# Down projection of a decoder layer: steps run in pairs, product by product, with sums kept in PSUM

## The chip, the cores and the metric

The kernel runs on one core of a Trainium2 chip. The metric is the time of the whole program on the device in microseconds (us); of several executions the median is taken. The core's engines are TensorE (PE in the profile: matrix products, sums kept in PSUM banks of 128x512 f32), VectorE (DVE), ScalarE (ACT), GpSimd (POOL) and SyncE (SP, which here only issues DMAs). All but PE read and write SBUF; DVE and ACT also read PSUM.

## The reference

One layer of a decoder, batch 1, 1024 positions, width 1024, in f32:

```
h = rmsnorm(x); proj = h @ w_in
o = [rmsnorm(fox_attention), rmsnorm(stick_breaking_attention)]     # 8 + 8 heads of 64
x = x + o @ w_out
h = rmsnorm(x)
u = causal_dwconv(h @ w_up, conv_w, conv_b)                         # 1024 -> 2 x 2816, width 3
gate, val = split(u)
x = x + (silu(gate) * val) @ w_down                                 # 2816 -> 1024
out = rmsnorm(x)
```

The change concerns the last product, `(silu(gate) * val) @ w_down`, and the addition of x to it.

## The kernel before

Everything is held transposed: rows of a tile are features, columns are positions. An f32 matrix product is made of three matmuls on halves split as high + low part (`mm3`, L158 to L161: high x high, low x high, high x low). `wh` is the high part of a weight, cast by ACT (L904), and `wl` the low part, raw minus high, a subtraction on DVE or POOL (L906). The operands (b11, t2, t4, ... with h and l) are split in the same way by ACT (L760) and DVE or POOL (L761).

Up and down projection use a 2x2 block scheme with seven products in place of eight, and sums on both sides. A step is one pair of output row blocks: seven products, named in `PORD` (L49) by the weight block or weight sum they use: a11, s2, a22, a12, s1, s3, s4. Their other operand is, in that order, b11, t2, t4, b21, t1, t3, b22. The weight sums s1, s2, s3, s4 are made by POOL (L878, L879, L885, L886) from the raw weights `wraw`, which come by DMA from HBM (L863), in a pool of 2 buffers; the sums stand in the pool `sp_` with one buffer each.

- Up: 22 steps (`NJ`), products of 4 x 3 = 12 matmuls each. For each step the four outputs are put together by DVE, convolved (L1003), gated (L1098, `tg`), and stored in HBM as operands of the down projection (`td`).
- Down: the inner dimension comes in three chunks (`KN` = 4, 3, 3 blocks) and each chunk has four steps, 12 steps in all: 28 products of 12 matmuls and 56 of 9. After that comes a small plain part for the last two blocks (`plain`), and the final norm.

The loop over down steps (L1126 on) makes, for each product in the order of `PORD`, one call of `product`, which takes a fresh PSUM bank (`bank`, six of pool ps_u and two of ps_p in turn). Its result is added into the accumulators `y[m, c]` in SBUF by DVE. A copy of a11's result (`m1s`, by ACT) and a running sum `u2` serve several outputs; a step has 11 additions on DVE. The accumulators are loaded with x from HBM in `load_y` (L1118). Their pool `fin` takes the memory of the pool `up`, which the up phase and the staging of the operands of chunk 0 have used, so that the loads wait for the last use of it.

In the last step of the up phase and of a chunk, `operands` loads the operand for product n of the next chunk right after the last product n of the old one, through six staging buffers (`ua`, `ffr`, `m1s`), since the operands have one buffer each. `ahead_to(idx + 4)` has the weights of a product split four products ahead of its matmuls, in pair tiles for two products, three of them; which engine takes a `wl` stands in `produce`.

SP issues its DMAs in program order (L72). The order on the other engines is made by a scheduler, which may move instructions within their dependences.

Of the kernel before, what the change touches and what calls it, by code (L numbers as in the profile page):

```python
# [9 lines left out]
F32 = mybir.dt.float32  # L10
# [3 lines left out]
ALU = mybir.AluOpType  # L14
# [3 lines left out]
P = 128  # L18
# [8 lines left out]
NPRE = 3  # L27
# [41 lines left out]
def layer(ctx, tc, xT, wqk, wv0, wv, wout, wup, wdn, cols, fbias, yT):  # L69
# [3 lines left out]

    const = ctx.enter_context(tc.tile_pool(name="const", bufs=1))
    dram = ctx.enter_context(tc.tile_pool(name="dram", bufs=1, space=DRAM))
    wraw = ctx.enter_context(tc.tile_pool(name="wraw", bufs=2, side="right"))
    wspl = ctx.enter_context(tc.tile_pool(name="wspl", bufs=3, side="right"))

    ident = const.tile([P, P], F32, name="ident")
# [75 lines left out]
                    if d == 1:  # L155
                        n.split(min(n.pieces, int(frac * n.pieces + 0.01)))

    def mm3(ps, ah, al, bh, bl, start, stop):  # L158
        nc.tensor.matmul(ps, ah, bh, start=start, stop=False)  # L159
        nc.tensor.matmul(ps, ah, bl, start=False, stop=False)  # L160
        nc.tensor.matmul(ps, al, bh, start=False, stop=stop)  # L161

    small = ctx.enter_context(tc.tile_pool(name="small", bufs=4))

# [551 lines left out]

    x2x = ExitStack()
    b1p = ctx.enter_context(tc.tile_pool(name="b1p", bufs=1))
    sp_ = ctx.enter_context(tc.tile_pool(name="sp_", bufs=1))
    x2p = x2x.enter_context(tc.tile_pool(name="x2p", bufs=1))  # L720
    ps_u = ctx.enter_context(tc.tile_pool(name="ps_u", bufs=6, space=PSUM))

# [91 lines left out]
    tp_ = ctx.enter_context(tc.tile_pool(name="tblk", bufs=1, side="right"))  # L814
    t2, t4, t1, t3, b22 = (halves(tp_, n) for n in ("t2", "t4", "t1", "t3", "b22"))

    def product(w, o, b, n=4):
        ps = bank()
        wh, wl = w
        for k in range(n):  # L820
            sl = slice(o + k * P, o + (k + 1) * P)
            mm3(ps, wh[:, sl], wl[:, sl], b[k][0], b[k][1], k == 0, k == n - 1)
        return ps

    steps = [("u", j, 4) for j in range(NJ)] + [(c, mp, KN[c]) for c in range(NCH) for mp in range(KT // 2)]
# [18 lines left out]
    first(1)  # L844
    first(2)

    stream = [(j, n) for j in range(NS) for n in PORD if j >= NPRE or n not in ("a11", "a12")]
    made, tiles, plain = {}, {}, {}
    pos = [0]

# [272 lines left out]
    spare = [t[n] for n in range(KN[1], 4) for t in (b11, t2, t4, b21, t1, t3)]  # L1123
    rest = {}

    for s in range(NJ, NS):  # L1126
        c, mp, kn = steps[s]
        ev, od_ = 2 * mp, 2 * mp + 1
        for n in PORD:
            ahead_to(idx + 4)  # L1130
            if s == NS - 1 and n == PORD[3]:
                plain_split(0)
            if s == NS - 1 and n == PORD[-1]:
                plain_split(1)
            w, o = made[s, n]
            idx += 1
            ps = product(w, o, bmat[n], kn)
            if c == 0 and n == PORD[0]:
                if mp == 0:
                    load_y(0)  # L1140
                elif mp < KT // 2 - 1:
                    load_y(mp + 1)
            if c == 0 and mp == 0 and n == PORD[3]:
                load_y(1)
            if n == "a11":
                m1s = fin.tile([P, 512], F32, name="m1s")
                nc.scalar.copy(m1s, ps)
                tt(y[ev, 0], y[ev, 0], m1s, ALU.add)
            elif n == "s2":
                u2 = fin.tile([P, 512], F32, name="u2")  # L1150
                tt(u2, ps, m1s, ALU.add)
                tt(y[ev, 1], y[ev, 1], u2, ALU.add)
            elif n == "a22":
                tt(y[od_, 0], y[od_, 0], ps, ALU.subtract)
            elif n == "a12":
                tt(y[ev, 0], ps, y[ev, 0], ALU.add)
            elif n == "s1":
                tt(y[od_, 1], ps, y[od_, 1], ALU.add)
                tt(y[ev, 1], ps, y[ev, 1], ALU.add)
            elif n == "s3":  # L1160
                tt(u2, ps, u2, ALU.add)
                tt(y[od_, 1], y[od_, 1], u2, ALU.add)
                tt(y[od_, 0], y[od_, 0], u2, ALU.add)
            elif n == "s4":
                tt(y[ev, 1], ps, y[ev, 1], ALU.add)
            if mp == KT // 2 - 1 and c < NCH - 1:
                operands(n, c + 1, False)
            if c == 1 and mp == 1 and kind[n] < 4:
# [126 lines left out]
```

## Time and profile before

| | |
|---|---|
| median of 3 runs | 1442.48 us (1440.78 to 1443.48) |
| profiled execution | 1441.58 us, of which the span is 1439.6 us |
| mean granted clock of TensorE | 0.964 |
| busy, share of the span | PE 92%, DVE 78%, POOL 60%, ACT 43% |
| DMA queues by kind | hardware_dynamic 193.04 + 0.64 MB, instruction 0.85 + 0.36 MB |

The page's shares are averages over stages: the input projection and attention up to about 736 us, the up projection from there to 1174, the down projection to 1394, and the plain part with the final norm to 1440. Times on the span's scale start at 0 with the first instruction. A timeline row has the start, the time of one, engine, line, operation, output<-inputs, and in brackets how long the engine stood idle before and which work ended it. A wait row has engine, line, what was waited for, us in total, times, and the longest. In the table of stretches the clock is the share of full speed that TensorE was granted.

### The profile page before, as it was taken

What the parts mean: (1) busy time and instruction counts of PE and PEld (TensorE: products, weight loads), DVE (VectorE), ACT (ScalarE), POOL (GpSimd) and SP (SyncE); (2) the same over time, 40 slices, a digit from 0 to 9 for tenths busy, and PEclk for the clock granted to TensorE, in tenths of its full rate; (3) what the DMA queues carried; (4) which work ended last, traced back from release to release, by engine and by line L of the source; (5) the groups of instructions that cost most, each with busy time, mean ns of one, the idle gap of its engine ahead of it and who ended that gap; (6) DMA issues with size and microseconds to landing.
All of it is one profiled execution on the core that took longest, in us unless ns stands there. A gap on an engine that the chain in (4) does not pass through costs nothing.

```text
span 1439.6 us, 19147 instructions
## 1 busy us (share of the span) xinstructions
PE 1317.6 (92%) x6640; PEld 1075.9 (75%) x6640; DVE 1116.7 (78%) x1588; ACT 620.8 (43%) x1128; POOL 859.4 (60%) x730
## 2 busy tenths in 40 slices
PE   7899999999898887889778899999999998999995
PEld 5878878877787765777556688888888865878785
DVE  6246555655676677786899999998888889899987
ACT  5134434444454554353443434443443354344334
POOL 7344454543747573455667788878878763454423
PEclk9999999999999999999889999999999998999997
DMA  5556555545444454547311233333322355554313
GB/s 179 183 161 187 152 154 163 147 147 135 149 121 124 119 159 143 179 147 270 125 44 59 84 106 110 110 110 110 110 97 95 96 176 204 180 171 132 126 36 117
DMA packets 97232, 194.89 MB, mean 135 GB/s; under 512 B 8680, under 2 KB 35688, under 8 KB 97136
## 3 DMA queue, kind: packets, MB, share of 16 engines
q1 hardware_dynamic: 96272, 193.04, 42.6%
q8 instruction: 52, 0.85, 0.3%
q10 hardware_dynamic: 864, 0.64, 0.1%
q14 instruction: 44, 0.36, 0.1%
HBM read 132.79 MB, written 60.85 MB: 135 GB/s over the span
## 4 chain that ended last, share of the span: by engine, by line
PE 50%; DMA 18%; DVE 16%; POOL 7%; issue 6%; SPq 2%; ACT 2%; DVEq 0%; POOLq 0%; ACTq 0%
PE u L161 8%; PE u L160 8%; PE u L159 8%; PE pj L159 5%; PE pj L161 5%; PE pj L160 5%; DMA q<-qkd 4%; DVE fbt L493 3%; DMA vd<-vs 3%; DMA wraw<-in_wqk_dram 2%; DMA wraw<-in_wv_dram 2%; PE tp L505 2%; DMA fbt<-nfd 2%; PE o L526 2%; PE o L525 1%
## 5 line engine op out<-in xcount | busy, mean ns | idle before, releaser
L143 POOL TENSOR_TENSOR wl<-wraw,wh 128x256 fp32r<-128x256 f32 (+2 forms) x134 | 125.3, 952 | 26.9 <-ACT wh L140 21.3
L494 POOL TENSOR_TENSOR w<-w,fbt 128x128 f32<-128x128 f32 (+3 forms) x64 | 90.1, 1417 | 84.4 <-DVE fbt L493 59.9
L904 ACT CAST wh<-s 128x512 fp32r<-128x512 f32 (+1 forms) x136 | 79.8, 591 | 125.7 <-POOL s L879 71.0
L493 DVE TENSOR_TENSOR_SCAN fbt<-fbt 128x128 f32<-128x128 f32 (+3 forms) x64 | 103.5, 1624 | 25.9 <-ACT fbt L480 22.0
L142 POOL TENSOR_SCALAR wh<-wraw 128x256 fp32r<-128x256 f32 (+1 forms) x112 | 55.3, 509 | 108.8 <-DMA wraw<-in_wqk_dram 60.7
L878 POOL TENSOR_TENSOR s<-wraw 128x512 f32<-128x512 f32 (+1 forms) x34 | 55.8, 1641 | 96.0 <-DVE wl L906 53.5
L505 PE MATMUL tp<-ident,w 128*128 128x128 f32 x576 | 94.0, 281 | 19.5 <-DVE pl L514 9.5
L159 PE MATMUL pj<-xh,wh 128*128 128x512 f32 x224 | 103.1, 460 | 5.1 <-DVE yf L293 5.1
L906 POOL TENSOR_TENSOR wl<-wraw,wh 128x512 fp32r<-128x512 f32 x60 | 102.9, 1722 | 0.6 <-ACT wh L904 0.6
L505 PEld LDWEIGHTS tp<-ident,w 128*128 128x128 f32 x576 | 70.7, 144 | 39.1 <-DVE pl L514 12.6
L906 POOL TENSOR_TENSOR wl<-s,wh 128x512 fp32r<-128x512 f32 x48 | 88.5, 1845 | 13.8 <-ACT wh L904 13.4
L514 DVE TENSOR_TENSOR pl<-tp,ph 128x512 fp32r<-128x512 f32 x96 | 64.9, 685 | 40.9 <-ACT ph L513 40.5
L161 PE MATMUL pj<-xh,wl 128*128 128x512 f32 x224 | 91.9, 410 | 0.0
L160 PE MATMUL pj<-xl,wh 128*128 128x512 f32 x224 | 91.3, 407 | 0.0
L485 ACT ACTIVATE w<-w,m 128x128 f32<-128x128 f32 (+3 forms) x64 | 49.7, 776 | 91.1 <-DVE m L475 86.0
L1003 DVE SCALAR_TENSOR_TENSOR tg<-ua,col,tg 128x1023 f32<-128x1023 f32 (+1 forms) x44 | 88.1, 2002 | 0.0
L480 ACT ACTIVATE fbt<-s 128x512 f32<-128x512 f32 (+2 forms) x96 | 47.8, 498 | 83.8 <-PE s L470 39.2
L489 POOL TENSOR_SCALAR w<-w,l 128x128 f32<-128x128 f32 (+3 forms) x64 | 47.6, 748 | 59.9 <-DVE l L488 32.7
L904 ACT CAST wh<-wraw 128x512 fp32r<-128x512 f32 (+1 forms) x96 | 55.1, 589 | 63.1 <-DMA wraw<-in_wdn_dram 25.0
L1003 DVE SCALAR_TENSOR_TENSOR tv<-ub,col,tv 128x1023 f32<-128x1023 f32 (+1 forms) x44 | 76.0, 1727 | 5.7 <-ACT tv L1001 5.6
L513 ACT CAST ph<-tp 128x512 fp32r<-128x512 f32 x96 | 55.7, 590 | 53.1 <-PE o L525 33.4
L885 POOL TENSOR_TENSOR s<-wraw 128x512 f32<-128x512 f32 (+1 forms) x34 | 56.4, 1658 | 35.7 <-DVE wl L906 33.4
(409 smaller groups left out, 4569.4 us busy)
## 6 DMA issues: line engine op xcount, KB each, us to landing
wraw<-in_wup_dram SPq DMA_DIRECT2D x47, 512.0 KB, 3.6
qkd<-hl SPq DMA_DIRECT2D x32, 512.0 KB, 2.9
td<-tg SPq DMA_DIRECT2D x44, 256.0 KB, 2.3
vd<-vs SPq DMA_DIRECT2D x32, 256.0 KB, 4.5
q<-qkd SPq DMA_DIRECT2D x16, 512.0 KB
kh<-qkd SPq DMA_DIRECT2D x32, 256.0 KB, 16.6
kl<-qkd SPq DMA_DIRECT2D x32, 256.0 KB, 17.4
vt<-vd SPq DMA_DIRECT2D x16, 512.0 KB, 17.9
```

The costliest lines, as they stand in the source:

```text
L143: nc.gpsimd.tensor_tensor(self.lo[:, sl], self.raw[:, sl], f32(self.hi[:, sl]), ALU.subtract)
L159: nc.tensor.matmul(ps, ah, bh, start=start, stop=False)
L160: nc.tensor.matmul(ps, ah, bl, start=False, stop=False)
L161: nc.tensor.matmul(ps, al, bh, start=False, stop=stop)
L493: nc.vector.tensor_tensor_scan(qt[:, rev], qt[:, rev], qt[:, rev], 1.0, ALU.mult, ALU.bypass)
L494: nc.gpsimd.tensor_tensor(w[:, :n], w[:, :n], qt[:, T - n + 1:T + 1], ALU.mult)
L505: nc.tensor.transpose(tp[:, a * 256 + b * P:a * 256 + (b + 1) * P], ws[2 * g + b][:, kb * P:(kb + 1) * P], ident)
L514: nc.vector.tensor_tensor(pl[:, z:], tp[:, z:], f32(ph[:, z:]), ALU.subtract)
L885: nc.gpsimd.tensor_tensor(d["s3"], g[:, :w], v[:, :w], ALU.subtract)
L904: nc.scalar.copy(h[:, o:o + w], src)
L906: eng.tensor_tensor(l[:, o:o + w], src, f32(h[:, o:o + w]), ALU.subtract)
L1003: nc.vector.scalar_tensor_tensor(t[:, s:], us[:, :T - s], col[:, cw + tap:cw + tap + 1], t[:, s:], op0=ALU.mult, op1=ALU.add)
```

## The change

Two down steps of a chunk (two pairs of output row blocks) form a unit, and go product by product: product n of the first step, product n of the second, then the next n. The order of the products is new (`PORD_D`). Three of the seven go on accumulating in a bank that another product has begun (`ONTO`): s2 on a11's, s4 on s1's, s3 on a11's again. The copy `m1s` and the sums `u2` go: a step has 8 additions on DVE, and no ACT copy. The products a22 and a12 take banks of ps_p, the others of ps_u. y is loaded in the first unit, at positions 0, 1, 6 and 10. Raw weights of both steps of the next unit are asked for at a12. `wraw` gets four buffers and `sp_` two, and the DMA scratch of the program is set to 1024. The number of matmuls is the same.

```diff
+PORD_D = ("a11", "a22", "s1", "s2", "a12", "s4", "s3")
+ONTO = {"s2": "a11", "s4": "s1", "s3": "a11"}
-    wraw = ctx.enter_context(tc.tile_pool(name="wraw", bufs=2, side="right"))
+    wraw = ctx.enter_context(tc.tile_pool(name="wraw", bufs=4, side="right"))
-    sp_ = ctx.enter_context(tc.tile_pool(name="sp_", bufs=1))
+    sp_ = ctx.enter_context(tc.tile_pool(name="sp_", bufs=2))
...
-    def product(w, o, b, n=4):
-        ps = bank()
+    def product(w, o, b, n=4, onto=None, pool=None):
+        ps = onto or (pool.tile([P, 512], F32, name="u" if pool is ps_u else "pj") if pool else bank())
...
-            mm3(ps, wh[:, sl], wl[:, sl], b[k][0], b[k][1], k == 0, k == n - 1)
+            mm3(ps, wh[:, sl], wl[:, sl], b[k][0], b[k][1], k == 0 and onto is None, k == n - 1,
+                onto is not None)
...
+    units = [(j,) for j in range(NJ)] + [(j, j + 1) for j in range(NJ, NS, 2)]
+    stream = [(j, n) for q in units for n in (PORD if q[0] < NJ else PORD_D) for j in q
+              if j >= NPRE or n not in ("a11", "a12")]
...
         if n == ("a12" if j >= NPRE else "a22"):
-            raws(j + 1)
+            for q in follow[j]:
+                raws(q)
...
+    for unit in units[NJ:]:
+        c, _, kn = steps[unit[0]]
+        last = steps[unit[-1]][1] == KT // 2 - 1
+        on = {}
+        for at, (n, s) in enumerate((n, s) for n in PORD_D for s in unit):
...
+            ps = on[s, n] = product(w, o, bmat[n], kn, on.get((s, ONTO.get(n))),
+                                    pool=ps_p if n in ("a22", "a12") else ps_u)
+            if c == 0 and unit[0] == NJ and at in (0, 1, 6, 10):
+                load_y((0, 1, 6, 10).index(at))
+            if n in ("a11", "a12"):
+                tt(y[ev, 0], ps, y[ev, 0], ALU.add)
             elif n == "a22":
                 tt(y[od_, 0], y[od_, 0], ps, ALU.subtract)
...
+            elif n in ("s2", "s4"):
+                tt(y[ev, 1], ps, y[ev, 1], ALU.add)
+            else:
                 tt(y[od_, 1], ps, y[od_, 1], ALU.add)
...
+                if n == "s3":
+                    tt(y[od_, 0], ps, y[od_, 0], ALU.add)
+            if s != unit[-1]:
+                continue
+            if last and c < NCH - 1:
                 operands(n, c + 1, False)
...
-    nc = _bacc.Bacc("TRN2", target_bir_lowering=False, num_devices=1)
+    nc = _bacc.Bacc("TRN2", target_bir_lowering=False, num_devices=1,
+                    dynamic_dma_scratch_size=1024)
```

The scheduler's order moves in three places that matter below. In the rows a name has the number of its buffer, so one name with one number is one piece of memory. `[waits ...]` names the engines and DMA queues whose progress an instruction waits for.

First, PE in the first down unit. Before, the second product of the first step, s2 on t2, has a bank of its own, `u_11322`, beside a11's `u_11300`:

```order
L159 MATMUL u_11300<-b11h3_7182,wh_11120 128x512 [waits Activation_49]
L160 MATMUL u_11300<-b11l3_7183,wh_11120 128x512 [waits DVE_49]
L161 MATMUL u_11300<-b11h3_7182,wl_11121 128x512
L159 MATMUL u_11322<-t2h0_7624,wh_11120 128x512 [waits Activation_49]
L160 MATMUL u_11322<-t2l0_7625,wh_11120 128x512 [waits Pool_49]
L161 MATMUL u_11322<-t2h0_7624,wl_11121 128x512
```

In the changed kernel s2 comes after a11, a22 and s1 of both steps, and writes into a11's bank, `u_11298` (`u_11409` is s1 of the second step):

```order
L164 MATMUL u_11409<-t1h2_7644,wl_11290 128x512
L162 MATMUL u_11409<-t1h3_7646,wh_11289 128x512
L163 MATMUL u_11409<-t1l3_7647,wh_11289 128x512
L164 MATMUL u_11409<-t1h3_7646,wl_11290 128x512
L162 MATMUL u_11298<-t2h0_7624,wh_11343 128x512 [waits DVE_49,Activation_49]
L163 MATMUL u_11298<-t2l0_7625,wh_11343 128x512
L164 MATMUL u_11298<-t2h0_7624,wl_11344 128x512 [waits Pool_49]
```

The first of these matmuls has a wait for DVE, since DVE reads the same bank.

Second, DVE in the same place: `b22l1` to `b22l3` are the last operands staged through the old memory, `tg` is the last gated block, and y0_0 the first accumulator. Before:

```order
L761 TENSOR_TENSOR t3l3_7655<-m1s_11227,t3h3_7654 128x512 [waits DMAHW0_49,Activation_49]
L1003 SCALAR_TENSOR_TENSOR tg_11270<-ua_11137,col_76,tg_11270 128x1022 [waits DVE_49]
L906 TENSOR_TENSOR wl_11339<-wraw_11235,wh_11338 128x512 [waits PE_49,DMAHW2_49,Activation_49,Pool_49]
L906 TENSOR_TENSOR wl_11379<-s2_11381,wh_11378 128x512 [waits PE_49,Activation_49]
L906 TENSOR_TENSOR wl_11379<-wraw_11233,wh_11378 128x512 [waits DMAHW1_49]
L1098 TENSOR_TENSOR tg_11270<-tg_11270,tv_11266 128x1024 [waits Activation_49]
L761 TENSOR_TENSOR b22l1_7659<-ua_11251,b22h1_7658 128x512 [waits DMAHW4_49,Activation_49]
L761 TENSOR_TENSOR b22l2_7661<-ffr_11258,b22h2_7660 128x512 [waits DMAHW5_49,Activation_49]
L761 TENSOR_TENSOR b22l3_7663<-m1s_11262,b22h3_7662 128x512 [waits DMAHW6_49,Activation_49]
```

In the changed kernel, from the same t3l to the add that reads a11's bank:

```order
L764 TENSOR_TENSOR t3l3_7655<-m1s_11224,t3h3_7654 128x512 [waits DMAHW2_49,Activation_49]
L764 TENSOR_TENSOR b22l1_7659<-ua_11244,b22h1_7658 128x512 [waits DMAHW4_49,Activation_49]
L764 TENSOR_TENSOR b22l2_7661<-ffr_11251,b22h2_7660 128x512 [waits DMAHW5_49,Activation_49]
L1017 SCALAR_TENSOR_TENSOR tg_11263<-ua_11141,col_76,tg_11263 128x1022 [waits DVE_49]
L764 TENSOR_TENSOR b22l3_7663<-m1s_11255,b22h3_7662 128x512 [waits DMAHW6_49,Activation_49]
L919 TENSOR_TENSOR wl_11290<-s1_11316,wh_11289 128x512 [waits Pool_49]
L1112 TENSOR_TENSOR tg_11263<-tg_11263,tv_11259 128x1024 [waits Activation_49]
L919 TENSOR_TENSOR wl_11344<-s2_11317,wh_11343 128x512 [waits PE_49,Pool_49]
L919 TENSOR_TENSOR wl_11382<-wraw_10995,wh_11381 128x512 [waits PE_49]
L919 TENSOR_TENSOR wl_11382<-wraw_10999,wh_11381 128x512
L1157 TENSOR_TENSOR y0_0_11273<-u_11298,y0_0_11273 128x512 [waits DMAHW3_49,DMAHW7_49,DVE_49,Pool_49]
```

The three b22l have moved ahead of the weight splits and the gate product, and the add into y0_0 reads the bank itself and stands behind four wl.

Third, POOL at the start of the up projection (`_7801` to `_7803` are the sums of step 0, `_7920` to `_7922` those of step 1). Before:

```order
L878 TENSOR_TENSOR s1_7801<-wraw_7797 128x512
L879 TENSOR_TENSOR s2_7802<-s1_7801,wraw_7799 128x512
L885 TENSOR_TENSOR s3_7803<-wraw_7799,wraw_7797 128x512
L906 TENSOR_TENSOR wl_7796<-s2_7802,wh_7795 128x512
L906 TENSOR_TENSOR wl_7796<-wraw_7797,wh_7795 128x512
L886 TENSOR_TENSOR s2_7802<-wraw_7799,s2_7802 128x512
L906 TENSOR_TENSOR wl_7902<-s2_7802,wh_7901 128x512
L878 TENSOR_TENSOR s1_7920<-wraw_7820 128x512
L906 TENSOR_TENSOR wl_7943<-wraw_7820,wh_7942 128x512
```

In the changed kernel:

```order
L898 TENSOR_TENSOR s3_7803<-wraw_7799,wraw_7797 128x512
L891 TENSOR_TENSOR s1_7920<-wraw_7820 128x512
L892 TENSOR_TENSOR s2_7921<-s1_7920,wraw_7822 128x512
L898 TENSOR_TENSOR s3_7922<-wraw_7822,wraw_7820 128x512
L919 TENSOR_TENSOR wl_7796<-s2_7802,wh_7795 128x512
L919 TENSOR_TENSOR wl_7796<-wraw_7797,wh_7795 128x512
L899 TENSOR_TENSOR s2_7802<-wraw_7799,s2_7802 128x512
L919 TENSOR_TENSOR wl_7902<-s2_7802,wh_7901 128x512
L919 TENSOR_TENSOR wl_7902<-s2_7921,wh_7901 128x512
L891 TENSOR_TENSOR s1_8032<-wraw_7946 128x512
L899 TENSOR_TENSOR s2_7921<-wraw_7822,s2_7921 128x512
L919 TENSOR_TENSOR wl_7943<-wraw_7820,wh_7942 128x512
```

Three sums of step 1 now stand ahead of the first wl of step 0, and `wl_7943` (a22 of step 1) has s1 of step 2 and s4 of step 1 ahead of it. PE's own order is the same in the up projection.

## Rows read from the trace of the kernel before

**Rows 1.** The page's chain that ended last, shares of the span by engine.
```profile
PE 50%; DMA 18%; DVE 16%; POOL 7%; issue 6%; SPq 2%; ACT 2%; DVEq 0%; POOLq 0%; ACTq 0%
```

**Rows 2.** Table of stretches, PE: from:to, length, busy (matmuls), clock, DMA share, GB/s.
```profile
738.00:774.00 36.00, 26.71 (x84) 0.81 0.17 59
804.00:828.00 24.00, 19.68 (x75) 0.93 0.35 118
830.00:1174.00 344.00, 344.00 (x1481) 1.00 0.32 107
1174.00:1231.00 57.00, 47.03 (x169) 0.91 0.60 208
1231.00:1282.00 51.00, 51.00 (x221) 1.00 0.55 180
1394.00:1440.00 46.00, 29.47 (x186) 0.82 0.26 92
```

**Rows 3.** Timeline of PE: start, us of one, engine, line, operation, operands.
```profile
1174.31 0.39 PE L159 MATMUL u<-b11h,wh 128*128 128x512 f32 x1
1195.05 0.63 PE L159 MATMUL u<-t1h,wh 128*128 128x512 f32 x1
1231.27 0.40 PE L159 MATMUL u<-b11h,wh 128*128 128x512 f32 x1
1332.33 0.40 PE L159 MATMUL u<-t2h,wh 128*128 128x512 f32 x1
1350.31 0.40 PE L159 MATMUL u<-b11h,wh 128*128 128x512 f32 x1
```

**Rows 4.** Waits of PE, 1205 to 1400: line, releaser, us in total, times, longest.
```profile
PE pj L161 <- DVE wl L906: 2.9, 2, 2.7
PE pj L160 <- POOL b22l L761: 1.1, 1, 1.1
```

**Rows 5.** Waits of SP's DMA queue, 1150 to 1216.
```profile
SPq L1118 <- DVE b22l L761: 9.0, 1, 9.0
```

**Rows 6.** Timeline of SP's DMA queue at the loads of y.
```profile
1212.97 0.32 SPq L1118 DMA_DIRECT2D y<-x2f  x1
```

**Rows 7.** Timeline of DVE around the transition to the down projection.
```profile
1198.54 0.68 DVE L761 TENSOR_TENSOR t3l<-m1s,t3h 128x512 fp32r<-128x512 f32 x1
1200.94 1.76 DVE L761 TENSOR_TENSOR t3l<-m1s,t3h 128x512 fp32r<-128x512 f32 x1
1202.63 2.29 DVE L1003 SCALAR_TENSOR_TENSOR tg<-ua,col,tg 128x1022 f32<-128x1022 f32 x1
1208.80 2.30 DVE L1098 TENSOR_TENSOR tg<-tg,tv 128x1024 f32<-128x1024 f32 x1
1215.78 0.69 DVE L1148 TENSOR_TENSOR y<-y,m1s 128x512 f32<-128x512 f32 x1
```

**Rows 8.** Timeline of POOL at the start of the up projection.
```profile
735.00 1.75 POOL L885 TENSOR_TENSOR s<-wraw 128x512 f32<-128x512 f32 x1
738.54 1.81 POOL L906 TENSOR_TENSOR wl<-s,wh 128x512 fp32r<-128x512 f32 x1 [1.80 <-ACT wh L904]
747.93 9.53 POOL L906 TENSOR_TENSOR wl<-s,wh 128x512 fp32r<-128x512 f32 x1 [4.21 <-ACT wh L904]
757.43 1.71 POOL L878 TENSOR_TENSOR s<-wraw 128x512 f32<-128x512 f32 x1
```

**Rows 9.** Waits of PE, 738 to 774.
```profile
PE pj L161 <- POOL wl L906: 3.0, 1, 3.0
```

**Rows 10.** Waits of PE, 804 to 828.
```profile
PE pj L161 <- POOL wl L906: 2.2, 1, 2.2
PE u L161 <- DVE wl L906: 1.4, 1, 1.4
PE u L161 <- POOL wl L906: 0.5, 1, 0.5
```

**Rows 11.** Waits of POOL, 730 to 832.
```profile
POOL s L878 <- DMA wraw<-in_wup_dram: 9.5, 3, 3.7
```

More of the change, by code (lines that the diff above doesn't have):

```diff
@@ L156, in ahead, with mm3 @@
                         n.split(min(n.pieces, int(frac * n.pieces + 0.01)))
[L158 to L161, printed above, removed]
+    def mm3(ps, ah, al, bh, bl, start, stop, more=False):
+        nc.tensor.matmul(ps, ah, bh, start=start, stop=False, skip_group_check=more)
+        nc.tensor.matmul(ps, ah, bl, start=False, stop=False, skip_group_check=more)
+        nc.tensor.matmul(ps, al, bh, start=False, stop=stop, skip_group_check=more)
     small = ctx.enter_context(tc.tile_pool(name="small", bufs=4))
@@ L845, in layer @@
     first(2)
-    stream = [(j, n) for j in range(NS) for n in PORD if j >= NPRE or n not in ("a11", "a12")]
+    units = [(j,) for j in range(NJ)] + [(j, j + 1) for j in range(NJ, NS, 2)]
+    stream = [(j, n) for q in units for n in (PORD if q[0] < NJ else PORD_D) for j in q
+              if j >= NPRE or n not in ("a11", "a12")]
+    follow = {}
+    for q, r in zip(units, units[1:] + [(NS,)]):
+        if len(q) == len(r):
+            follow.update({j: (i,) for j, i in zip(q, r)})
+        else:
+            follow.update({j: () for j in q})
+            follow[q[-1]] = r
     made, tiles, plain = {}, {}, {}
@@ L1124, in layer @@
     rest = {}
[L1126 to L1129, printed above, removed]
+    for unit in units[NJ:]:
[3 more added lines that the diff above has]
+        for at, (n, s) in enumerate((n, s) for n in PORD_D for s in unit):
+            mp = steps[s][1]
+            ev, od_ = 2 * mp, 2 * mp + 1
             ahead_to(idx + 4)
[L1131 to L1134, printed above, removed]
+            if s >= NS - 2 and at in (10, 12):
+                plain_split(at // 2 - 5)
@@ L1135, in layer @@
             w, o = made[s, n]
             idx += 1
[L1137 to L1152, printed above, removed]
+            ps = on[s, n] = product(w, o, bmat[n], kn, on.get((s, ONTO.get(n))),
+                                    pool=ps_p if n in ("a22", "a12") else ps_u)
@@ L1153, in layer @@
+            if c == 0 and unit[0] == NJ and at in (0, 1, 6, 10):
+                load_y((0, 1, 6, 10).index(at))
+            if n in ("a11", "a12"):
+                tt(y[ev, 0], ps, y[ev, 0], ALU.add)
             elif n == "a22":
                 tt(y[od_, 0], y[od_, 0], ps, ALU.subtract)
-            elif n == "a12":
-                tt(y[ev, 0], ps, y[ev, 0], ALU.add)
-            elif n == "s1":
+            elif n in ("s2", "s4"):
+                tt(y[ev, 1], ps, y[ev, 1], ALU.add)
+            else:
@@ L1158, in layer @@
                 tt(y[od_, 1], ps, y[od_, 1], ALU.add)
[L1159 to L1166, printed above, removed]
+                if n == "s3":
+                    tt(y[od_, 0], ps, y[od_, 0], ALU.add)
@@ L1167, in layer @@
+            if s != unit[-1]:
+                continue
+            if last and c < NCH - 1:
                 operands(n, c + 1, False)
-            if c == 1 and mp == 1 and kind[n] < 4:
+            if c == 1 and not last and kind[n] < 4:
                 i = kind[n]
```

## The prediction, made before the changed kernel ran

> **What bounds the kernel now.** I read the chain of waits first. Half of the path that sets the end is TensorE (PE), and DMA, VectorE (DVE) and GpSimd (POOL) share most of the rest [rows 1]. A chain over the whole span mixes stages, so I went to the table of stretches next [rows 2]. From 830 to 1174, the steady part of the up projection, PE is busy in every microsecond: 1481 matmuls in 344.00 us, 0.232 each. The same holds between the first two and the last two row pairs of the down projection, 1231 to 1282. There nothing can be won but by fewer matmuls, and the change takes none away. What is left for it are the stretches where PE is not full: 738 to 774 and 804 to 828 (start of the up projection), 1174 to 1231 (up to down), and, inside the down projection, the two places where the operands of the next chunk arrive. The tail from 1394 on runs the same instructions in both kernels and is counted at nothing, and so are the stages before 736.
>
> The excess of a stretch is its length less its matmuls at 0.2326 us (a product of 12 matmuls is 2.79, of 9 matmuls 2.09):
> - Up to down: the first matmul of the first down step starts at 1174.31 and that of the third at 1231.27 [rows 3]; two steps are 14 products, 39.1 us, so 57.0 - 39.1 = 17.9 us are stalls, nearly all of them for operands of chunk 0 that are loaded and split late.
> - Chunk 0 to 1: PE waits 1.1 us for b22l of POOL ([rows 4], a wait of that size).
> - Chunk 1 to 2: from 1332.33 to 1350.31 there are six products of nine, 12.6 us, in 17.98 [rows 3]: 5.4 us, of which 2.7 is one wait for a weight split `wl` on DVE [rows 4] and the rest what follows it.
> - Up start: 36 - 84 x 0.2326 = 16.5 us and 24 - 75 x 0.2326 = 6.55 us [rows 2].
>
> **The change part by part.** Of 840 down matmuls none goes. DVE loses 36 adds and ACT 12 copies; at 0.68 us an add (the short ones of [rows 7]) that is 24 us of DVE work, but in the full stretches DVE is not waited for, so there the gain is nothing: PE covers it.
>
> *The chunk changes.* Before, an operand's last use by one chunk and its first use by the next are six or seven products apart, and in that time DVE must split it, beside the weights and 11 adds a step. Now 12 or 13 products lie between, and 8 adds a step go with them. The rows show waits of 1.1 and 2.7 us; the distance grows by six products of 2.09 us, 12.5 us. I take both away: -1.1 - 5.4 = -6.5. The other end is 0, if DVE as a whole is what is late there.
>
> *The transition up to down.* The first unit has one new tie: product s2 goes on accumulating in the bank of a11, so PE may not start it before DVE has added that bank into y0_0. That add needs y0_0, whose load needs memory that the last staged operand still uses. Before, the SP queue stood 9.0 us for that operand (b22l of DVE) [rows 5] and issued the load at 1212.97 [rows 6]; the add that reads it started at 1215.78 [rows 7], 2.8 us later. No matmul stood behind this add then, since every product had a bank of its own. Now PE is in order behind s2.
> In the new order b22l comes earlier on DVE. From 1202.63, the end of the last t3l: 0.68 + 0.68 + 2.29 (conv) + 0.68 = 1206.96 for the third b22l, 2.8 for the load: 1209.8. DVE meanwhile works through what its order puts ahead of the add: four wl at 0.68 and the gate product at 2.30, 5.02 us: 1211.98. The add, 0.69, ends at 1212.7 (0.68, 2.29, 2.30 and 0.69 are in [rows 7]). Six of the 14 products are done by then (they need 16.7 us from 1174.31 and as much waiting as before), eight are left, 22.3 us: 1235.0. PE has stood and restarts at the lower clock, which in 804 to 828 cost (1 - 0.93) x 24 = 1.7 us [rows 2]: 1236.7 against 1231.27, **+5.4**. Behind the waiting add on DVE stand the adds of y1_0 and y1_1, that of y2_0 (which holds the other step's s2), and the wl of s4; they pass within a few 0.68 us.
> Bounds: without those wl and without a slow clock the add ends 1210.5 and the unit 1232.8, +1.5. It cannot be a gain: t1 of the second step needs a wl that stands behind the third b22l, 1206.96 + 0.68 + 11 matmuls = 1210.2, so s2 is not ready earlier. At the other end two b22l and four wl take 1.76 like the contended t3l at 1200.94 [rows 7] rather than 0.68: 6 x 1.08 = 6.5 more, +11.9. I take the 0.68, since POOL has little to do there.
>
> A sentence on the clock: matmuls of t1 at 1195.05, after PE's waits for operands, took 0.63 us against 0.39 at 1174.31 [rows 3], that is the lower of the two levels (1.2 and 2.4 GHz). The Trainium skill, page "TensorE: Matmul & The Clock Gate", section "What's actually happening", says that the throttled state is the default and that activity releases it, so the whole first product behind the gate would run there: 12 x 0.24 = 2.9 in place of 1.7, and the time would be 1.2 us more. The trace agrees in kind; no run here shows that very place.
>
> *Later accumulations.* From the second unit on, y is there, and six products (12.5 us or more) lie between the first product in a bank and the next one on it, against one add of 0.68. Nothing.
>
> *Up start.* PE's order is the same, POOL's is not: with two buffers for the weight sums, POOL makes s1, s2, s3 of step 1 before the first wl of step 0. Two sides:
> (a) Cost. Three sums of 1.71 to 1.75 (as at 735.00 and 757.43 [rows 8]) run beside the DVE work that PE waits for; three DVE operations at 1.76 instead of 0.68 are +3.2. At the next tie, where PE waited 3.0 us for a wl of POOL [rows 9], two more POOL operations stand ahead of the wl of a22 of step 1: 2 x 1.71 = 3.4. Together 6.6, the upper end. The lower is 0: POOL stood idle 1.80 before the wl at 738.54 and 4.21 before that at 747.93 [rows 8], 6.0 us in which 5.2 us of sums fit.
> (b) Gain. Between 804 and 828 PE waited 2.2 + 0.5 for POOL's wl and 1.4 for DVE's [rows 10], while POOL waited three times, 9.5 us in all, for weights from HBM [rows 11]. With four raw buffers the weights of a step come a step earlier and POOL is ahead by a set of sums. I take the whole 6.55 away; the other end is 0.
> I take both at their full size: the POOL operation at 747.93 that took 9.53 us [rows 8] beside a run of DVE operations says that the two engines hold each other up at just this place, so I do not call the sums free. Net +0.05.
>
> *The rest.* Raw weights for two steps are asked for together, some ten products (20 us and more) before they are used: nothing. The splits of the plain part move within the last unit: nothing. The smaller DMA scratch: the queues that move data are hardware queues by the page's list; nothing.
>
> Sum on the profiled execution's own 1441.58 us (span 1439.6): +5.4 - 6.5 + 0.05 = -1.05, 1440.5. The median of the runs shown, 1442.48, is 0.9 above it, so the forecast is **1441.5: no change**. A measurement of this kernel can tell about 0.2%, 2.9 us, from none.
>
> **Rivals.**
> 1. *The sums are free* (faster). POOL fits them into its 6.0 idle us and the waits at 804 to 828 go: +5.4 - 6.5 - 6.55 = -7.65, 1434.8. For it: those idle times [rows 8]. Against it: the 9.53.
> 2. *POOL and DVE hold each other up at the up start, and nothing comes back* (slower). The place is 738 to 774, the price 6.6, and it decides from the point at which the sums of step 1 run against DVE operations with two SBUF inputs; the waits at 804 to 828 stay, as POOL keeps its whole load. +5.4 - 6.5 + 6.6 = +5.5, 1448.0. For it: t3l 0.68 and 1.76, wl 9.53 [rows 7, 8]. Against it: POOL's waits for DMA [rows 11], which more buffers shorten. Beside it a rule: the Trainium skill, page "SBUF — State Buffer", section "Who interferes with whom", says that a DVE instruction with two SBUF inputs contends with a GpSimd instruction that reads SBUF, that the lock is exclusive and the loser blocks. By it the 5.2 us of sums are never free beside these operations, and rival 1 falls; the trace agrees in the two durations, but does not show which operations of the new order meet.
> 3. *The gate at the transition is long* (slower). The contended end, +11.9: +11.9 - 6.5 + 0.05 = +5.45, 1447.9. For it: the t3l at 1200.94 took 1.76. Against it: the add at 1215.78 took 0.69 [rows 7].
> 4. *The chunk waits stay* (the change gives the operands room but they are late for DVE's sake): +5.4 + 0.05, 1447.9. For it: the 2.7 us wait is for DVE's wl, not an operand. Against it: DVE has 36 adds less.
>
> **How the numbers follow.** Forecast 0.36 (own range 1439.6 to 1445), rival 1 0.34, rival 2 0.14, rival 3 0.10, rival 4 0.06. The range 1434.2 to 1448.8 reaches into rival 1 on one side and rivals 2 to 4 on the other, and leaves out about 0.2 where their sizes are beyond the values worked out. Faster by over 0.2%: 0.34; within: 0.36; slower: 0.30.
>
> **What would show it.** Transition: a PE wait for DVE's add into y0_0 ahead of the first t2 product on a11's bank, and the first a11 of the second unit 59 to 66 us after the first down matmul (57.0 before). Chunk changes: no PE waits for wl or b22l after that. Up start: the excess of 738 to 774 grows by up to 6.6 and that of 804 to 828 goes. The forecast is wrong if 738 to 774 keeps its 16.5 us while 804 to 828 loses its 6.55 (rival 1), or if PE's wait at the gate is absent or beyond 10 us.

## The result, and the profile after

The changed kernel took 1458.59 us (median of 4 runs, 1458.32 to 1460.12) against 1441.63 for the kernel before in the same session: a ratio of 1.0118, with a 95% interval of 1.0101 to 1.0136. It is 17 us slower. The forecast was no change, 1441.5, with a range that ended at 1448.8.

The span of the profiled execution is 1456.8 us (1439.6 before). The chain that ended last has changed its owner; before, PE held half of it [rows 1]:

```profile
DVE 31%; PE 28%; DMA 19%; issue 10%; POOL 4%; ACT 4%; SPq 3%; DVEq 0%; ACTq 0%; POOLq 0%
```

The stretches of PE, to be held against [rows 2] (from:to, length, busy (matmuls), clock, DMA share, GB/s):

```profile
738.00:774.00 36.00, 20.88 (x57) 0.72 0.18 59
804.00:828.00 24.00, 23.46 (x102) 1.00 0.45 165
845.00:1165.00 320.00, 313.61 (x1336) 1.00 0.26 97
1191.00:1252.00 61.00, 47.13 (x169) 0.83 0.75 262
1252.00:1409.00 157.00, 156.48 (x673) 1.00 0.34 109
1409.00:1457.00 48.00, 31.37 (x186) 0.80 0.25 88
```

The third line is the surprise. The steady part of the up projection, which was full before, has lost 6.4 us of PE's busy time within 320. The second line shows the opposite: 804 to 828, with 75 matmuls before, has 102 now, so the waits of [rows 10] have gone from that place. But the first has 57 matmuls in place of 84. The waits of PE in three parts follow: 728 to 850, 850 to 1165, and the transition, 1189 to 1252 (us in total, times, longest). The second fence is whole; the first has the three largest of its part, the third the two that matter below and one more:

```profile
PE pj L164 <- POOL wl L919: 6.9, 2, 6.4
PE u L162 <- ACT wh L917: 4.7, 1, 4.7
PE u L164 <- POOL wl L919: 4.2, 2, 3.5
```

```profile
PE u L164 <- DVE wl L919: 2.9, 3, 1.2
PE u L164 <- POOL wl L919: 2.5, 5, 0.5
PE pj L164 <- POOL wl L919: 1.0, 2, 0.5
```

```profile
PE u L164 <- DVE wl L919: 8.6, 1, 8.6
PE u L162 <- ACT b11h L763: 1.7, 1, 1.7
PE u L162 <- DVE y L1157: 0.2, 1, 0.2
```

For the second and third chunk there is only this left, in place of the 2.9 us of [rows 4]:

```profile
PE pj L164 <- DVE wl L919: 0.4, 1, 0.4
```

Where the 17.2 us of span came from is best seen in lengths between fixed points of PE's own timeline, and in stalls, which are the length less 0.2326 us for each matmul (the 20 small ones of a norm at the start of the up projection are counted too):

| part | predicted | measured | how measured |
|---|---|---|---|
| ahead of the first up product | 0 | +1.0 | its start, 704.11 and 705.08 |
| up start | +0.05 | +4.5 | stalls in the first 500 up matmuls, 35.9 and 40.4 |
| up, steady | 0 | +9.5 | stalls in the next 1344, none and 9.5 |
| up to down | +5.4 | +5.5 | 17.9, and 21.4 with 2.0 ahead of the first matmul |
| chunk changes | -6.5 | -5.7 | 6.6 and 0.9 |
| plain part and final norm | 0 | +2.3 | 45.4 and 47.6 |

The two parts that the new loop is about, transition and chunk changes, came out near the prediction, -0.2 together (-1.1 predicted); all parts make 17.1 of the 17.2. The loss lies ahead of them, in code that the change to the loop doesn't touch, and in the tail. The 1.0 ahead of the first up product means nothing: in the kernels of the next section, which all leave the stages before it alone, that product starts anywhere from 702.9 to 709.1.

### The profile page after: what moved, and what is told of

Read it like the earlier page. It is cut to its first block, busy times and chain, and to the rows that moved or that the text cites. A ratio compares the mean times of both kernels' runs of the same rounds, so it can differ in the third digit from the quotient of the medians.

```text
span 1456.8 us, 19096 instructions
## 1 busy us (share of the span) xinstructions
PE 1321.9 (91%) x6640; PEld 1077.9 (74%) x6640; DVE 1106.2 (76%) x1552; ACT 611.3 (42%) x1116; POOL 872.4 (60%) x730
## 4 chain that ended last, share of the span: by engine, by line
DVE 31%; PE 28%; DMA 19%; issue 10%; POOL 4%; ACT 4%; SPq 3%; DVEq 0%; ACTq 0%; POOLq 0%
DVE tg L1017 6%; DMA q<-qkd 5%; PE u L164 3%; PE u L163 3%; PE u L162 3%; DVE tv L1017 3%; PE pj L162 3%; PE pj L164 3%; DVE fbt L496 3%; PE pj L163 3%; DMA vd<-vs 3%; DMA wraw<-in_wqk_dram 2%; DVE tg L1112 2%; DMA wraw<-in_wv_dram 2%; DVE wl L919 2%
## 5 line engine op out<-in xcount | busy, mean ns | idle before, releaser
L891 POOL TENSOR_TENSOR s<-wraw 128x512 f32<-128x512 f32 (+1 forms) x34 | 59.8, 1758 | 66.7 <-DMA wraw<-in_wup_dram 22.0
L919 DVE TENSOR_TENSOR wl<-s,wh 128x512 fp32r<-128x512 f32 (+1 forms) x88 | 90.6, 1044 | 4.4 <-ACT wh L917 4.4
L1017 DVE SCALAR_TENSOR_TENSOR tv<-ub,col,tv 128x1023 f32<-128x1023 f32 (+1 forms) x44 | 83.5, 1899 | 8.7 <-ACT tv L1015 7.6
L483 ACT ACTIVATE fbt<-s 128x512 f32<-128x512 f32 (+2 forms) x96 | 47.6, 496 | 85.8 <-PE s L473 39.0
L469 PE MATMUL s<-kh,q 128*128 128x256 f32 (+2 forms) x192 | 69.1, 362 | 9.4 <-DMA kh<-qkd 7.5
L280 PE MATMUL pj<-wh,xh 128*128 128x256 f32 (+1 forms) x256 | 77.6, 303 | 0.0
## 6 DMA issues: line engine op xcount, KB each, us to landing
kh<-qkd SPq DMA_DIRECT2D x32, 256.0 KB, 16.5
```

The source lines that it names most:

```text
L280: nc.tensor.matmul(ps[:, :n], xh[k][:, sl], h, start=(k == 0), stop=False)
L469: nc.tensor.matmul(s[:, :cn], qb, kh[:, c0:c0 + cn], start=True, stop=False)
L1017: nc.vector.scalar_tensor_tensor(t[:, s:], us[:, :T - s], col[:, cw + tap:cw + tap + 1], t[:, s:], op0=ALU.mult, op1=ALU.add)
```

## The experiments

All times are from PE's timeline of one profiled execution of each kernel: *up* from the first matmul of the first up product to the first down matmul, *down* from there to the plain part, *tail* from there to the end of the span. The stalls of the up projection are given for the first 500 matmuls (to about 860) and for the next 1344; the last 24 are in neither. The last column is the ratio to the kernel before in the same session, where it was timed more than once; b_s2x2, b_s1x2, b_s3x2 and b_s13x2 were executed once. a_split, a_wlpool, a_copy and a_both run the up projection in one and the same order, and their 469.9 to 472.7 show what a difference there has to exceed.

| kernel | up | stalls, first 500 / next 1344 | down | tail | span | ratio |
|---|---|---|---|---|---|---|
| before | 470.2 | 35.9 / 0 | 219.9 | 45.4 | 1439.6 | |
| changed | 486.4 | 40.4 / 9.5 | 217.7 | 47.6 | 1456.8 | 1.0118 |
| b_pools | 484.6 | 40.4 / 8.2 | 223.3 | 45.2 | 1459.9 | 1.0115 (1.0091 to 1.0139) |
| b_sums2 | 482.2 | 35.6 / 9.9 | 222.0 | 46.1 | 1453.6 | 1.0074 (1.0056 to 1.0091) |
| a_sums1 | 468.7 | 34.4 / 0 | 228.9 | 48.1 | 1454.2 | 1.0070 (1.0057 to 1.0084) |
| a_split | 470.7 | 36.3 / 0 | 214.9 | 46.7 | 1437.7 | 0.9959 (0.9940 to 0.9979) |
| b_s2x2 | 470.8 | 34.2 / 1.4 | 221.1 | 46.0 | 1441.5 | |
| b_s1x2 | 469.1 | 34.8 / 0 | 220.7 | 46.0 | 1441.9 | |
| b_s3x2 | 470.9 | 36.6 / 0 | 220.7 | 46.0 | 1443.9 | |
| b_s13x2 | 480.0 | 37.7 / 5.9 | 223.0 | 45.3 | 1452.1 | |
| a_lo3 | 490.2 | 52.0 / 2.2 | 217.0 | 46.7 | 1456.8 | 1.0091 (1.0058 to 1.0123) |
| a_wlpool | 470.9 | 36.6 / 0 | 219.3 | 48.3 | 1444.0 | 1.0019 (1.0008 to 1.0030) |
| a_copy | 469.9 | 35.6 / 0 | 213.4 | 47.6 | 1438.4 | 0.9963 (0.9950 to 0.9976) |
| a_both | 472.7 | 38.4 / 0 | 210.0 | 48.4 | 1440.2 | 0.9948 (0.9928 to 0.9968) |

### Is it the pools, and which of them?

**b_pools**: the kernel before, with only the pools and the DMA scratch of the change.

```diff
-wraw ... bufs=2      +wraw ... bufs=4
-sp_ ... bufs=1       +sp_ ... bufs=2
+dynamic_dma_scratch_size=1024
```

> The kernel before with only the pools of the change: four raw weight buffers, two sets of sums, the smaller DMA scratch; the down loop is the old one. Both theories (A: the second set of sums lets POOL make sums ahead of the splits that PE waits for; B: with four raw buffers SP no longer stands at the weight loads but at the stores of tg, and the loads come late and in fours) expect the whole loss of the up projection: first down matmul at about 1189.5 in place of 1174.3, time about 1457. If the loss comes from the twin steps after all, it stays at 1442.

Up 484.6: 14.4 of the 16.2 us that the up projection lost are there without the twin steps.

**b_sums2**: the kernel before, with `sp_` at two buffers and the DMA scratch of 1024. (The expectation says that the scratch is as before; the kernel that ran has the smaller one. The scratch alone can't be the cause: b_s1x2 and b_s3x2 below have it too, and lose nothing.)

> The kernel before with two sets of sums alone (raw buffers two, scratch as before). Theory A (order of POOL): the up projection loses by itself, first down matmul at 1180 to 1189, time 1447 to 1457. Theory B (loads behind stores on SP): two raw buffers keep the old loads, so nothing changes: 1442, first down matmul at 1174.

Up 482.2: the second set of sums costs 12.0 us, all of it behind the first 500 matmuls. One wait of 2.3 us for a wl of DVE, at 855, and the lower clock behind it are 4.2 of them; the rest is spread over the steady part. The orders of PE, DVE and SP are word for word those of before; only POOL and ACT differ.

**a_sums1**: the changed kernel with `sp_` back at one buffer.

> The changed kernel with one set of sums again (raw buffers four). Theory A: POOL's order in the up projection is that of before, the waits of PE for wl in 850 to 1165 go, first down matmul near 1174, time about 1443. Theory B: the four raw buffers alone are to blame, so it stays near 1458, first down matmul near 1189.

Up 468.7: four raw buffers do no harm. Theory B of these runs, the loads held up behind stores, falls on both. The time is not 1443, though: with one set of sums, two interleaved steps have to take turns in it (in the down projection POOL stood 84.5 us before a sum for DVE to read the old one), and the down projection is 228.9. That was overlooked in the expectation.

**a_split**: two raw buffers and one set of sums in the up projection, second ones under other tags for the second step of a unit.

```diff
+tag=("wraw", "wraw2")[j >= NJ and (j - NJ) % 2]
+tag=n + ("", "b")[j >= NJ and (j - NJ) % 2]
```

> The changed kernel with the room used only in the down projection: the up projection has two raw buffers and one set of sums as before, the second step of a unit has tags of its own for both. Both theories: first down matmul back at 1174, the down projection as in the changed kernel (219.6 us from first matmul to the plain part), time 1441 to 1444, depending on whether the 2.3 us that the tail lost come back.

Up is back at 470.7, down is 214.9, 5.0 under the kernel before, and the kernel is faster than both. What the changed loop itself is worth is seen here.

### Why does a second set of sums cost 12 us?

DVE, 860 to 1150, before and then in the changed kernel. The columns of the stretch are length, and then busy time (instructions) of PE, PEld, DVE, ACT and POOL, clock, DMA share and GB/s:

```profile
860.00:1150.00 290.00, 290.00 (x1249) 235.03 (x1248) 260.97 (x234) 117.01 (x163) 234.29 (x143) 1.00 0.31 103
```

```profile
860.00:1150.00 290.00, 284.12 (x1211) 226.72 (x1209) 259.83 (x224) 110.12 (x159) 241.25 (x138) 1.00 0.26 97
```

DVE's busy time is the same, but it got through 224 instructions in place of 234: 1.160 us each, not 1.115. What DVE waited for, before (the three largest of seven) and after:

```profile
DVE x L1055 <- DMA td<-x: 8.8, 7, 1.5
DVE u L1083 <- PE u L161: 5.7, 7, 1.3
DVE ua L1090 <- PE u L161: 3.1, 4, 0.8
```

```profile
DVE x L1069 <- DMA td<-x: 19.3, 7, 3.8
DVE tv L1017 <- ACT tv L1015: 5.0, 7, 0.7
```

Before, DVE waited for PE (also on two rows for `pj`, 1.6 each): 12.0 us of the 290, the only time it had to spare. In the changed kernel it never waits for PE: its own chain of operations and waits has run out of room. Two things filled it. At 1.160 us in place of 1.115 the 224 instructions took some 10 us more, and the waits for its own stores and for ACT grew from 14.9 to 28.4 us; together that is more than 12.0. The operations that had grown have two inputs in SBUF; the gate product, which has two as well, had shrunk. Before and after (x count, busy us, mean ns):

```profile
L906 DVE TENSOR_TENSOR wl<-s,wh 128x512 fp32r<-128x512 f32 x30 | 27.5, 917 | 0.0
L1003 DVE SCALAR_TENSOR_TENSOR tv<-ub,col,tv 128x1022 f32<-128x1022 f32 x15 | 26.4, 1758 | 0.0
L1098 DVE TENSOR_TENSOR tg<-tg,tv 128x1024 f32<-128x1024 f32 x15 | 31.6, 2108 | 4.7 <-ACT tg L1097 4.7
```

```profile
L919 DVE TENSOR_TENSOR wl<-s,wh 128x512 fp32r<-128x512 f32 x29 | 43.9, 1513 | 0.0
L1017 DVE SCALAR_TENSOR_TENSOR tv<-ub,col,tv 128x1022 f32<-128x1022 f32 x14 | 32.4, 2311 | 0.0
L1112 DVE TENSOR_TENSOR tg<-tg,tv 128x1024 f32<-128x1024 f32 x15 | 22.3, 1487 | 4.1 <-ACT tg L1111 4.1
```

And what had kept the wl short before is a wait of POOL that looked like waste. With one set of sums POOL may not write the next s1 or s3 until DVE has read the old one for its wl:

```profile
POOL s L885 <- DVE wl L906: 25.3, 15, 1.8
POOL s L878 <- DVE wl L906: 13.8, 5, 2.9
```

In those 39 us POOL stood still while DVE made the wl: of the 30 wl of this stretch 22 had no POOL instruction beside them and took 0.68 us. In the changed kernel 7 of 28 had none; the other 21 took 1.76 to 1.79. Yet POOL hardly stands still less in all. Its waits in the stretch come to 54.2 us before, 46.9 in the changed kernel and 55.8 in b_sums2. In the last two they are mainly for DMA and for DVE's gate product, and fall beside other operations of DVE. In a_sums1 the waits are back, and so is the up time (in order the two lines answer to these):

```profile
POOL s L898 <- DVE wl L919: 28.2, 16, 1.8
POOL s L891 <- DVE wl L919: 19.1, 8, 2.8
```

In b_sums2 they are gone, and the same two DVE groups are long, and PE waits for a wl:

```profile
L906 DVE TENSOR_TENSOR wl<-s,wh 128x512 fp32r<-128x512 f32 x29 | 35.2, 1212 | 0.0
L1003 DVE SCALAR_TENSOR_TENSOR tv<-ub,col,tv 128x1022 f32<-128x1022 f32 x15 | 34.8, 2319 | 0.0
```

```profile
PE u L161 <- DVE wl L906: 3.0, 4, 1.6
```

Two theories were left: A, that the order in which POOL makes the sums is what PE pays for, and B, that the lost waits are. (This B is not that of the first four runs, which has fallen.) Four runs tell them apart.

**b_s2x2, b_s1x2, b_s3x2, b_s13x2**: in the kernel before, two buffers for s2 alone, s1 alone, s3 alone, and s1 and s3.

```diff
-d[n] = sp_.tile([P, 512], F32, name=n)
+d[n] = sp_.tile([P, 512], F32, name=n, bufs=2 if n == "s2" else 1)
```

> The kernel before with the smaller scratch and two buffers for s2 alone. In POOL's order one sum more stands ahead of the wl of the last product of the step before, in every step (with all three sums doubled: one more in one step and two in the next). Theory (PE pays for the number of sums that POOL makes first): about two thirds of the 12 us that doubling all three cost, first up product to first down product 476 to 480 us. Rival (it is the second buffer of any of them, or its place in memory): 482 as with all three, or 470 as before if s3 is the one that counts.

> The kernel before with the smaller scratch and two buffers for s1 alone: POOL's order in the steady up projection is that of before, but POOL no longer waits at s1 for the wl of DVE that reads the old s1 (13.8 us of such waits before, beside 25.3 at s3). Theory A (PE pays for the order): nothing, first up product to first down product 470 us. Theory B (POOL's waits for DVE keep the two engines from working against each other; without them DVE's operations take their contended times, and DVE falls behind): DVE's wl grow from 0.92 us on the mean to about 1.0, the waits at s3 still hold, 470 to 473.

> The same with two buffers for s3 alone. POOL's order changes little (s3 goes one place ahead), and the larger of the two waits goes. Theory A: nothing to 2 us, 470 to 472. Theory B: DVE's wl on the mean 1.0 to 1.1 us, a first loss, 470 to 476.

> Two buffers for s1 and for s3, one for s2: both waits of POOL for DVE's wl go, while the order of POOL in the steady part is that of the run with s3 alone, with no sum more ahead of a wl than there. Theory A: as with s3 alone, 470 to 472. Theory B: DVE's wl at 1.1 to 1.3 us, DVE falls behind, PE waits for wl again, 475 to 482.

b_s2x2 moves one sum ahead of a wl in every step and costs nothing (470.8), though DVE's waits for PE are gone in it: theory A in its simple form, a price for each sum put ahead, is out. b_s1x2 and b_s3x2 cost nothing either. b_s13x2, with POOL's order in the steady part hardly other than in b_s3x2 (s1 and s3 of every second step change places), costs 9.8 us (480.0), as B expected. But it is not the lost waits that set it apart. They are gone in b_s3x2 too, where POOL, from 860 to 1150, waits for DMA only:

```profile
POOL s L885 <- DMA wraw<-in_wup_dram: 47.9, 15, 5.2
POOL s L878 <- DMA wraw<-in_wup_dram: 3.7, 5, 0.9
```

The groups of DVE in b_s3x2 and then b_s13x2:

```profile
L906 DVE TENSOR_TENSOR wl<-s,wh 128x512 fp32r<-128x512 f32 x30 | 36.2, 1208 | 0.0
L1003 DVE SCALAR_TENSOR_TENSOR tv<-ub,col,tv 128x1022 f32<-128x1022 f32 x15 | 21.2, 1411 | 0.0
```

```profile
L906 DVE TENSOR_TENSOR wl<-s,wh 128x512 fp32r<-128x512 f32 x29 | 35.2, 1214 | 0.0
L1003 DVE SCALAR_TENSOR_TENSOR tv<-ub,col,tv 128x1022 f32<-128x1022 f32 x15 | 34.9, 2330 | 0.0
```

So B as I wrote it is too simple: the wl is as long in b_s3x2, which loses nothing, as in b_s13x2. In b_s3x2 the convolutions came out short, and DVE still waited 16.5 us for PE; in b_s13x2 it never did. Neither a lost wait nor a long wl decides. What goes with the loss is that DVE's time to spare is used up, by its operations as they happen to fall against POOL's and by its own waits: in the changed kernel, b_pools, b_sums2 and b_s13x2 DVE does not wait for PE once. Why two second buffers together move the operations so, where each alone does not, no run shows.

**a_lo3**: a direct test of DVE as the limit, in the changed kernel: the wl of s1 goes to POOL.

```diff
-LO_UP = ("s3", "s1")
+LO_UP = ("s3",)
```

> The changed kernel, with the weight split of s1 in the up projection on POOL instead of DVE (one wl per step: 15 in 290 us). DVE spends about 22 us of 290 on these, POOL would spend about 25 and stood idle 49. Theory B (DVE is the one engine that has run out of time in the up projection, since its operations take their contended times): PE's waits for DVE's wl go, DVE waits for PE again, first up product to first down product 470 to 476 in place of 486.4, time 1443 to 1449. Theory A (POOL makes sums before the wl that PE waits for): POOL gets still more ahead of those wl, the waits for POOL's wl grow, 486 or more, time 1458 or more.

The expectation of B for the total was missed (490.2), and the run is worth the more for it, since the two parts went opposite ways. In the steady part the loss goes from 9.5 to 2.2, although POOL has more to do (267 us, 241 before): 1242 matmuls from 860 to 1150, where the changed kernel had 1211, and DVE waits for PE again:

```profile
860.00:1150.00 290.00, 289.46 (x1242) 233.48 (x1242) 256.76 (x211) 112.43 (x162) 267.47 (x153) 1.00 0.26 96
```

```profile
DVE ua L1104 <- PE u L164: 1.9, 3, 0.8
```

At the start the stalls rise from 40.4 to 52.0. PE's waits for a wl of POOL behind 820 grow from 0.5 and 3.5 to 3.1 and 5.0, and those for DVE's splits of t2 and t4 from 2.0 to 6.7. So the 4.5 us of the changed kernel's start are in the main POOL's: PE waited 6.4 us at once for a wl of POOL, where it was 3.0 before [rows 9], and 3.5 for another at 832. To these comes a wait of 4.7 for a wh of ACT, 1.5 before, which ACT cast after it had waited for an operand of DVE. The 9.5 us of the steady part are DVE's. More than half of PE's waits there are for POOL's wl (3.5 of 6.4), but POOL itself stood 29.6 us for DVE's gate product, and in b_sums2 all of PE's waits are for DVE. The start needs both pools: b_sums2 and a_sums1, with one each, have no loss in their first 500 matmuls, b_pools has 4.5.

### What holds the transition?

The changed kernel's DVE from the last b22l to the add into y0_0, and PE at the same time:

```profile
1222.78 0.68 DVE L764 TENSOR_TENSOR b22l<-m1s,b22h 128x512 fp32r<-128x512 f32 x1
1223.38 0.68 DVE L919 TENSOR_TENSOR wl<-s,wh 128x512 fp32r<-128x512 f32 x1
1224.05 1.23 DVE L1112 TENSOR_TENSOR tg<-tg,tv 128x1024 f32<-128x1024 f32 x1
1228.08 0.68 DVE L1157 TENSOR_TENSOR y<-u,y 128x512 f32<-128x512 f32 x1
```

```profile
1224.12 0.79 PE L164 MATMUL u<-t1h,wl 128*128 128x512 f32 x1 [8.59 <-DVE wl L919]
1224.71 0.63 PE L162 MATMUL u<-t1h,wh 128*128 128x512 f32 x1
1229.97 0.39 PE L162 MATMUL u<-t2h,wh 128*128 128x512 f32 x1
```

PE waited 8.6 us for the wl of s1 that DVE made at 1223.38, ended s1, and then waited 0.2 us more for the add that reads the bank of a11: two ties that end together. Of the clock: after the wait the matmuls took 0.63 us for nine in a row (the one at 1224.71 is the first) and 0.39 from 1229.97 on; the granted clock was 0.50 from 1224.6 to 1228.6, the lower of the two levels (1.2 and 2.4 GHz), and 1.00 from 1229.9 to 1233. The Trainium skill, page "TensorE: Matmul & The Clock Gate", section "What's actually happening", has the throttled state as the default and says that activity releases it. The trace agrees, with 0.50 right behind the wait of 8.6 us and 1.00 later.

**a_wlpool**: a_split, with that wl (and s2's) on POOL. **a_copy**: a_split, with a11's result of the first unit copied out of its bank by ACT. **a_both**: both, and a12 of the first unit in ps_u.

```diff
-eng = nc.vector if j > NJ or n in ...
+eng = nc.vector if j > NJ + 1 or n in ...          # a_wlpool, a_both
+if n == "a11" and unit[0] == NJ:                   # a_copy, a_both
+    m1s = stg.tile([P, 512], F32, name="m1s", tag="full")
+    nc.scalar.copy(m1s, ps)
+    tt(y[ev, 0], m1s, y[ev, 0], ALU.add)
-pool=ps_p if n in ("a22", "a12") else ps_u
+pool=ps_p if n == "a22" or (n == "a12" and unit[0] > NJ) else ps_u   # a_both
```

> The changed kernel with the room kept to the down projection (as a_split), and the weight splits of the first unit's second step on POOL where step one's are. Theory: the start of s2 in the first unit is held by two ties that end within 0.3 us of each other, the wl of s1 (8.6 us on PE) and DVE's add of a11 into y0_0. With the wl gone the other holds: the wait of PE moves to the first t2 matmul (about 7 us for DVE's add), s2 starts at most 1 to 2 us earlier, time within 2 us of a_split. Rival: the wl was the only tie; then s2 starts about 8 us earlier and the time falls by 6 to 8.

> a_split with a11's bank of the first unit copied out by ACT, so that s2 need not wait for the load of y0_0. Theory (two ties): the wl of s1 still holds PE until the same time, s2 starts within 0.5 us of a_split, time within 1.5 us of it. Rival (the bank's read is what counts, as the prediction had it): s2 starts about 8 us earlier, time 6 to 8 less.

> Both at once, and a12 of the first unit in banks of ps_u, since the two of ps_p wait for y as well. Theory (two ties): s2 starts about 8 us earlier than in a_split (1203 in place of 1211 if its first down matmul stands at 1176), the down projection is 207 to 209 us in place of 214.9, the time 5 to 8 us under a_split and 9 to 14 under the kernel before. Rival: the loads of y, which go on being issued after the last b22l, hold s4 or a12 by then, and less than 3 us come back.

In a_wlpool the wait moved to the other tie, as expected, and grew, which was not:

```profile
PE u L162 <- DVE y L1157: 12.0, 1, 12.0
```

Its down projection is 4.4 us longer than a_split's, where a time within 2 us was expected. Its loads of y stood behind the gate product, which came later on DVE:

```profile
SPq L1132 <- DVE tg L1112: 13.1, 1, 13.1
```

a_copy did not test what it was meant to, since the scheduler moved PE's order as well: PE began s2 in the midst of s1 and came to the wl later, when DVE had nearly made it.

```profile
1200.98 0.80 PE L162 MATMUL u<-t2h,wh 128*128 128x512 f32 x1 [2.58 <-ACT m1s L1158]
1206.72 0.50 PE L164 MATMUL u<-t1h,wl 128*128 128x512 f32 x1 [0.64 <-DVE wl L919]
```

So s2 began 23.6 us after the first down matmul, in place of 35.1 in a_split. The theory had expected a change of at most 0.5 us, the rival 8 us. The down projection gained only 1.5 us by it; PE also stood 3.3 us at 1215 for an add of DVE (L1165).

In a_both s2 began after 25.3 us, 9.8 earlier than in a_split, and the down projection is 210.0, a little short of the 207 to 209 expected: 4.9 gained. What PE waits for there is the copy by ACT of the second step, which had stood 3.6 us for DVE's b22l:

```profile
PE u L162 <- ACT m1s L1158: 2.4, 1, 2.4
```

With the wl out of the way alone the add holds PE (a_wlpool), with both out of the way s2 starts some 10 us earlier (a_both): that is two ties. What the copy gives with PE's order unchanged, no run shows. a_both's time missed its expectation, with 6 us under the kernel before where 9 to 14 were expected. At 0.9948 it can't be told from a_split's 0.9959: in its profiled execution up and tail were 2.0 and 1.7 longer. Why the tail is 1 to 3 us longer in all kernels with the twin steps stays open; PE waits there for a DVE sum of squares, and no run was spent on it.

## Why the prediction was wrong, step by step

- *"There nothing can be won but by fewer matmuls"*, of the steady up projection, and *"in the full stretches DVE is not waited for, so there the gain is nothing"*: this is the step that failed. The sum has no term for that stretch, and it lost 9.5. The row of the stretch was read for PE alone. It says that nothing can be won, not that nothing can be lost: DVE stood at 261 of 290 us, and with its waits for stores and ACT (14.9) only 12.0 us were to spare. I looked at POOL's order where it changed first, at the start, and did not follow it to the steady part, where it is changed as well.
- *Up start, (a) and (b)*: a net of 0.05 forecast, +4.5 measured. Both sides came at their full size. In 738 to 774 the stalls grew by 6.3, mainly by two waits at the places that (a) had: 4.7 us for a wh in place of 1.5, and 6.4 for a wl in place of 3.0. In 804 to 828 they fell by 6.3. What the sum lacks is mainly a new wait behind that, 3.5 us for POOL's wl at 832, with the lower clock after it 5.0. That sums beside DVE are not free, which rival 2 had, was right. The Trainium skill, page "SBUF — State Buffer", section "Who interferes with whom", rules that a DVE instruction with two SBUF inputs contends with a POOL instruction that reads SBUF. The trace agrees with 0.92 us of wl on the mean before and 1.51 after, for the same instruction. The prediction held this rule against the start alone; in the steady part it would have pointed at the same two engines.
- *The transition*, +5.4: the size is right (+5.5), the path only in part, so the size is in part luck. The add ends about when predicted relative to b22l (5.3 us behind its end, 5.7 predicted), but s1's wl of the second step holds PE until the same moment, and PE's wait for the add itself was 0.2 us; I had that wl in the bound (1210.2) and not as a tie of its own. In a_split, where DVE came to the place earlier against PE, the transition costs 1.0 only:

```profile
1205.70 0.68 DVE L919 TENSOR_TENSOR wl<-s,wh 128x512 fp32r<-128x512 f32 x1
1206.35 1.23 DVE L1112 TENSOR_TENSOR tg<-tg,tv 128x1024 f32<-128x1024 f32 x1
1210.45 0.69 DVE L1157 TENSOR_TENSOR y<-u,y 128x512 f32<-128x512 f32 x1
```

  There the third b22l ends at about 1205.7 and the add at 1211.1, where the prediction had 1206.96 and 1212.7. The loads of y wait for the gate product (1207.58), not for b22l; in the changed kernel too, 9.8 us.
- *The chunk changes*, -6.5: right, -5.7; of the waits only 0.4 us is left.
- *The tail at nothing*: +2.3, not explained.
- Rival 2 had the right engines and the right kind of price, 1448.0, but its place was the start alone.

## What to carry to other kernels

The number of buffers in a pool sets not only who waits, but also which operations of two engines run side by side: before a pool is made larger, look at who will then run beside whom, and how much time the busier of the two has to spare. A stretch in which PE is full says that nothing can be won there, so ask next which engine has least slack in it, and add up its waits for PE: that is what a change may cost it before PE stands. (Here it was 12.0 us of 290; b_s2x2 used it up and lost next to nothing, b_s13x2 went beyond it.) And give more buffers to the stage that needs them, by a tag of its own, rather than to the pool.

## What the runs showed of the hardware

The same DVE subtraction, 128x512 with both inputs in SBUF, took 0.92 us on the mean in the steady up projection before and 1.51 in the changed kernel. The mean is of two values: 0.68 with no POOL instruction beside it, up to 1.79 with one. The convolution step of 1022 columns went from 1.76 to 2.31. DVE's adds from a PSUM bank stayed at 0.68 before and after, with POOL at work beside them. DVE's busy time does not show the contention: it was 261 and 260 us of 290.
